# A hybrid SSD and latent-attention decoder on one core: a fourth pair in the second round of the FFN's products, a norm moved behind transposes, and rope queries transposed one value tile earlier

## The chip, the core and the metric

The kernel runs on one core of one Trainium2 chip. A core has TensorE (PE, with its weight loads listed as PEld), VectorE (DVE), ScalarE (ACT), GpSimd (POOL) and SyncE (SP), which here issues DMAs. Each works through its own list of instructions in order, and they meet at semaphores. The metric is device time in microseconds (us). Three runs of the kernel before gave 1320.35, 1320.42 and 1320.91, a median of 1320.42. The profile is of a further execution, which took 1320.28.

## The reference

A residual stream `h` of 512 tokens by 1024 goes through two layers. The first mixes tokens with a Mamba-2 scan (SSD), the second with multi-head latent attention (MLA, 8 heads, queries and keys with a rope part of 64). Behind each mixer stands a norm, then a gated FFN of 2816 hidden channels with a causal convolution over 3 tokens, then a norm again:

```python
for i in range(DEPTH):
    if i < N_A_LAYERS:
        mix = ssd_mixer(h, ...)
    else:
        mix = mla_attention(h, ..., k_nope, k_rope, v, cos, sin)
    h = layer_norm(DN_ALPHA * h + mix, ln_mix_g[i], ln_mix_b[i])
    ff = conv_ffn(h, ffn_up[i], ffn_conv_w[i], ffn_conv_b[i], ffn_down[i])
    h = layer_norm(DN_ALPHA * h + ff, ln_ffn_g[i], ln_ffn_b[i])
    if i == N_A_LAYERS - 1:
        shared_kv = mla_shared_kv(h, ...)

def conv_ffn(h, up, conv_w, conv_b, down):
    u = causal_depthwise_conv(h @ up, conv_w, conv_b)
    g, val = jnp.split(u, 2, axis=-1)
    return (jax.nn.silu(g) * val) @ down
```

All is float32.

## The kernel before, in words

**Products.** Every operand of a large product is split into a high part and the rest, and a product is three matmuls: high by high, high by rest, rest by high (`mm_a`, L159, and `mm_b`, L165 to L167). `h` stays on the chip as four token tiles of 128. Its transposed copy `ht` comes from `transpose_h` (L245): 8 transposes per token tile on PE, two casts on ACT (L248) for the high part, two subtractions on DVE (L249) for the rest.

**Weights.** `WStream` streams all weights in a fixed order: SP issues each load into one of 6 buffers (`wst`, L54), ACT casts it to `wh` (L96), DVE subtracts to get `wl` (L97); there are 6 pairs of `wh` and `wl`. A load waits until the split of the weights 6 loads ahead has freed its buffer. `ahead` splits weights before they are wanted, `retire` gives a pair back.

**The FFN** (`ffn`). Up projections go by pairs of 128 channels (`ci`, 22 in all, one for the gate and one for the value): PE's matmuls, then convolution, silu and gate on ACT and DVE (`conv3_silu_gate`). There are two rounds. Within a round hidden tiles are joined to pairs, and `RP` says how many pairs a round has and in which groups: 5 in the first, 3 in the second. A pair and its two halves of output and tokens are multiplied in a scheme of 7 products in place of 8 (`pair_operands` builds the sums of hidden tiles on DVE and ACT, `down_pairs` multiplies; the sums of weights are made in the buffers `rs`, by loads that POOL issues with addition, and on DVE). The results are added to `h` (L352, L353). The 6 hidden tiles that are in no pair go through the **tail**: for each token tile `piece` runs two halves of 512 outputs, 3 matmuls for each of the 6 tiles (36 matmuls of 512 columns a token tile), using weight tiles that hold two hidden tiles of one half (6 of them).

**The tail's norm.** Behind each half `add_mix` adds PE's sum to `h` on DVE (L185). Then `ln_apply` runs a chain over three engines: the negative mean on DVE (L192), the Square with its sum on ACT (L194), two small steps to the reciprocal root on POOL (L195, L196), the gain on DVE (L199, twice), the bias on DVE (L202, twice). L199 needs the gain and bias, which `load_ln` (L172) fetches into `lngb`, 1024 KB broadcast over the partitions; SP issues it when its turn comes in SP's list, ahead of the tail. In the first FFN `transpose_h(i-1)` stands between tile i's matmuls and its norm, so PE goes from tile i's matmuls to the transposes of tile i-1 and on to tile i+1. Tile 3's are left to `pend`, which the next stage flushes. In the last FFN nothing is transposed; tile 3 ends in `ln_last`, which splits its second half into 256 and 256 (L216, L222), and the output goes out by DMA.

**The scan's end** (the last lines of `ssd`). Its last two groups of heads go into `h` for tiles 0 to 3 (`out_part`, L185), each tile followed by its norm; tile 0 is transposed in the iteration of tile 2, tile 1 in that of tile 3, and tiles 2 and 3 by `pend`, after the first matmuls of the FFN on tiles 0 and 1.

**MLA.** `qk(h)` makes a head's queries and keys, `qk_rope(h)` transposes the rope queries of two heads (4 transposes, L1166) and splits them (L1171 on DVE), `v_tile(i, hf)` makes one half of a token tile of the values, `scores(h)` multiplies (L1183).

**What sets the order.** The program is written stage by stage, and when it is built the instructions of each engine are put into one list, by an estimate of when each can run. An edge on an engine (`tc.issue_after(x)`) puts instructions of x's engine behind x in its list.

Of the kernel before, what the change touches and what calls it, by code (L numbers as in the profile page):

```python
# [14 lines left out]
ALU = mybir.AluOpType  # L15
# [102 lines left out]
class K:  # L118
# [118 lines left out]
    def transpose_h(self, i):  # L237

        nc = self.nc
        ts = slice(i * P, (i + 1) * P)  # L240
        for q in range(2):
            b = self.bank()
            for j in range(4):
                k = q * 4 + j
                nc.tensor.transpose(b[:, j * P:(j + 1) * P], self.h[:, i, k * P:(k + 1) * P], self.ident)  # L245
            bv = b.rearrange("p (k t) -> p k t", k=4)
            hi = self.htt[:, q * 4:(q + 1) * 4, 0, ts]
            nc.scalar.copy(hi, bv)  # L248
            nc.vector.tensor_tensor(self.htt[:, q * 4:(q + 1) * 4, 1, ts], bv, hi, op=ALU.subtract)  # L249

    def flush(self):
        for f in self.pend:
# [2 lines left out]

RP = ((2, 2, 1), (1, 1, 1))
R0 = 2 * sum(RP[0])
R1 = R0 + 2 * sum(RP[1])  # L260


def ffn_items(up, down):
# [5 lines left out]
    for r, ks in enumerate((range(R0), range(R0, HT))):  # L269
# [4 lines left out]
        for odd, hf, kinds in ((0, 0, "r"), (0, 1, "a"), (1, 1, "+="), (0, 0, "-"), (1, 0, None), (1, 0, "a")):  # L274
            j = ks[0]
            for p, n in enumerate(RP[r]):
                b = dv[:, j:j + 2 * n, hf * 512:(hf + 1) * 512].rearrange("p (k e) n -> p k e n", e=2)[:, :, odd, :]
# [106 lines left out]
def ffn(k, ws, base, cwp, gb, la=2, out=None, mid=None):  # L384

    nc, tc = k.nc, k.tc
    with ExitStack() as c:
# [12 lines left out]
        for r in range(2):  # L400
# [49 lines left out]
            if mid and not r:  # L450
                mid()
            n = down_pairs(k, ws, n, prs, RP[r], not r)
        k.load_ln(gb)
# [72 lines left out]
def ssd(k, ws, base, xT, x, cwp, hv, ngp, gb):  # L526
    nc, tc = k.nc, k.tc
    with ExitStack() as cx:
# [327 lines left out]
        def out_part(g, i, stats=False, retire=None):  # L856

            assert "rs" in G[g]
            w = [ws.get(n[0] + OFF[g] + j, 4 - j) for j in range(2)]
            for hf in range(2):  # L860
                b = k.bank()
                o = slice(hf * 512, (hf + 1) * 512)
                for j in range(2):
                    k.mm_b(b, G[g]["yT"][j], slice(i * P, (i + 1) * P), w[j][0][:, o], w[j][1][:, o], j == 0, j == 1)
                    if retire and hf == 1:
                        ws.retire(n[0] + OFF[g] + j)
                k.add_mix(i, hf, b, rstd[:, g, i:i + 1], stats)
# [89 lines left out]
        for i in range(NT):  # L957
            if i >= 2:
                out_part(NG - 2, i, retire=i == NT - 1)
            if i == NT - 1:  # L960
                k.transpose_h(1)
            out_part(NG - 1, i, stats=True, retire=i == NT - 1)
            if i == NT - 1:
                n[0] += 4
                ws.ahead(n[0], 2)
            if i == 2:
                k.transpose_h(0)
            k.ln_apply(i)
    k.pend = [lambda: k.transpose_h(NT - 2), lambda: k.transpose_h(NT - 1)]
    return n[0]  # L970

# [65 lines left out]
def mla(k, ws, base, ngp, gb):  # L1037
    nc, tc = k.nc, k.tc
    with ExitStack() as cx:
# [76 lines left out]
        def v_tile(i, hf, retire=False):  # L1116
            b = k.bank()
            wh, wl = ws.get(n[0] + voff[0] + hf)
            for kk in range(2):
                k.mm_b(b, cT[3 + kk], slice(i * P, (i + 1) * P), wh[:, kk * 512:(kk + 1) * 512], wl[:, kk * 512:(kk + 1) * 512], kk == 0, kk == 1)  # L1120
            if not V:
                V["t"] = k.htp.tile([P, KT, 2, SEQ], F32R, name="ht")
            v = V["t"][:, 2 * i + hf]
            nc.scalar.copy(v[:, 0], b)
            nc.vector.tensor_tensor(v[:, 1], b, v[:, 0], op=ALU.subtract)
            V[i, hf] = v
# [18 lines left out]
        def qk(h, off=0):  # L1145
            S = H.setdefault(h, {})
            w = [v[:, :640].rearrange("p (k m) -> p k m", k=5) for v in ws.get(n[0] + off)]
            bq, bk = k.bank(), k.bank()
            k.mm_a(bq, [v[:, 0:3] for v in w], cT[:3], slice(0, SEQ))
            k.mm_a(bk, [v[:, 3:5] for v in w], cT[3:], slice(0, SEQ))  # L1150
            if not off:
                ws.retire(n[0])
                n[0] += 1
                ws.ahead(n[0])

            for nm, b, sc in (("q", bq, SCALE), ("k", bk, 1.0)):
                t = one.tile([P, 2, SEQ], F32R, name=f"{nm}T")
                nc.scalar.activation(t[:, 0], b, AF.Copy, scale=sc)
                nc.vector.scalar_tensor_tensor(t[:, 1], b, sc, t[:, 0], op0=ALU.mult, op1=ALU.subtract)
                S[nm] = t  # L1160

        def qk_rope(h):
            if h % 2 == 0:
                b = k.bank()
                for i in range(NT):
                    nc.tensor.transpose(b[:, i * P:(i + 1) * P], qr[:, i, h * RD:(h + 2) * RD], k.ident)  # L1166
                for e in range(2):
                    t = one.tile([P, SEQ], F32R, name=f"qrT{e}")
                    s = b[e * RD:(e + 1) * RD, :]
                    nc.scalar.activation(t[:RD], s, AF.Copy, scale=SCALE)  # L1170
                    nc.vector.scalar_tensor_tensor(t[RD:], s, SCALE, t[:RD], op0=ALU.mult, op1=ALU.subtract)  # L1171
                    H.setdefault(h + e, {})["r"] = t
# [83 lines left out]
        n[0] += 2  # L1256
        voff[0] = 0
        qk(0, 2)
        v_tile(NT - 1, 0)
        qk_rope(0)  # L1260
        v_tile(NT - 1, 1)
        for j in range(3):
            ws.retire(n[0] + j)
# [31 lines left out]
def trunk_kernel(tc, *aps):  # L1295
    d = dict(zip(_INS, aps))
    out = aps[len(_INS)]
    with ExitStack() as ctx:
        ctx.enter_context(tc.manual_schedule(engines={mybir.EngineType.SP}))
        k = K(tc, ctx)  # L1300
        items = ssd_items(d['xbc'], d['zdt'], d['zw'], d['sow'])
        items += ffn_items(d['up'][0], d['down'][0])
        items += mla_items(d['dw'], d['vw'], d['rw'], d['hw'], d['aow'])
        items += ffn_items(d['up'][1], d['down'][1])
        ws = WStream(k, items, k.nb, 3, k.la)
        n = ssd(k, ws, 0, d['xT'], d['x'], d['cw4'], d['hv'], d['sng'], d['gb'][0])
        n = ffn(k, ws, n, d['cw3'][0], d['gb'][1], la=5, mid=lambda: rope_tables(k, d['pos'], d['freq']))
        n = mla(k, ws, n, d['ang'], d['gb'][2])
        n = ffn(k, ws, n, d['cw3'][1], d['gb'][3], out=out)
# [53 lines left out]
```

## Time and profile before

| | before |
|---|---|
| runs, us | 1320.35, 1320.42, 1320.91 (median 1320.42) |
| profiled execution, us | 1320.28 |
| its span, us | 1318.6 |
| granted TensorE clock, mean | 0.998 |
| PE busy | 1309.1 us, 99% |
| DVE busy | 998.0 us, 76% |
| ACT busy | 633.1 us, 48% |
| POOL busy | 99.9 us, 8% |
| bytes moved | 143.55 MB, mean 109 GB/s |

How to read the lines that follow. The time line has start, duration, engine, source line, operation, output and inputs, shape, count; in brackets the idle time of the engine before and what ended it. Rows of several instructions are joined. The chain lists start, duration, engine and line of the work that ended last. A row of PE's waits is what waited, for which engine and line, us in total, times, longest. A row of windows has the stretch, its length, then busy time and count of PE, PEld, DVE, ACT and POOL, the granted clock, the share of the DMA engines and GB/s. Times are from the start of the span.

The stages that the change touches lie here: the scan's end at 415 to 434, the first FFN's second round of up projections before 713, its products at 713 to 742, its tail at 742 to 777, MLA's first scores at 835, and the last FFN's tail from about 1279 to the end at 1318.6.

### The profile page before, as it was taken

How to read it: one execution, taken by the hardware profiler on the slowest of the kernel's cores; microseconds unless marked ns; L12 is line 12 of the kernel's file. 1: busy time of each engine (PE TensorE's matmuls, PEld its weight loads, DVE VectorE, ACT ScalarE, POOL GpSimd, SP SyncE). 2: the span in 40 equal slices, each digit the busy share in tenths (PEclk: the TensorE clock that was granted, in tenths of full speed). 3: DMA queues.
4: the chain of work that ended last, by engine and by line, in shares of the span. 5: the costliest groups of instructions: out<-in, count | busy, mean ns of one | idle time of the engine just before them, and what ended most of it. 6: DMA issues, size and time to landing. Idle time of an engine off the chain costs nothing.

```text
span 1318.6 us, 17522 instructions
## 1 busy us (share of the span) xinstructions
PE 1309.1 (99%) x6740; PEld 1106.3 (84%) x6740; DVE 998.0 (76%) x1539; ACT 633.1 (48%) x1030; POOL 99.9 (8%) x98
## 2 busy tenths in 40 slices
PE   9999999999999999999999999999999999999997
PEld 8888888888888988888888899888898888888886
DVE  7788898787798868866757776887577686666585
ACT  6665555446453544444443444665254444444341
POOL 0111011001011001000001022000100010000001
PEclk9999999999999999999999999999999999999999
DMA  8422313313410533352311721321044217332151
GB/s 295 178 112 113 120 45 140 128 58 132 163 65 1 179 128 81 80 205 98 112 48 33 247 86 61 111 82 33 32 147 136 80 31 216 128 96 81 33 176 64
DMA packets 49108, 143.55 MB, mean 109 GB/s; under 512 B 5344, under 2 KB 6368, under 8 KB 47488
## 3 DMA queue, kind: packets, MB, share of 16 engines
q1 hardware_dynamic: 44544, 134.04, 29.5%
q0 software_dynamic: 4480, 8.39, 3.9%
q8 instruction: 53, 0.87, 0.3%
q14 instruction: 31, 0.25, 0.1%
HBM read 140.25 MB, written 2.16 MB: 108 GB/s over the span
## 4 chain that ended last, share of the span: by engine, by line
PE 98%; DVE 1%; issue 0%; ACT 0%; DVEq 0%; ACTq 0%
PE ps L159 57%; PE ps L165 10%; PE ps L167 10%; PE ps L166 10%; PE ps L1183 2%; PE ps L733 1%; PE ps L1217 1%; PE ps L841 1%; PE ps L741 1%; PE ps L245 1%; PE ps L722 1%; PE ps L700 1%; PE ps L1204 1%; PE ps L674 1%; DVE wl L97 0%; PE ps L554 0%
## 5 line engine op out<-in xcount | busy, mean ns | idle before, releaser
L159 PE MATMUL ps<-ht,wh 128*128 128x512 f32 (+1 forms) x2272 | 518.7, 378 | 0.7 <-ACT ht L248 0.4
L159 PEld LDWEIGHTS ps<-ht,wh 128*128 128x128 f32 x2272 | 409.0, 188 | 79.9 <-ACT ht L248 0.8
L97 DVE TENSOR_TENSOR wl<-wst,wh 128x1024 fp32r<-128x1024 f32 (+4 forms) x226 | 254.9, 1145 | 38.3 <-ACT wh L96 38.0
L159 PE MATMUL ps<-ht,wl 128*128 128x512 f32 (+1 forms) x1136 | 267.3, 377 | 0.0
L96 ACT CAST wh<-wst 128x1024 fp32r<-128x1024 f32 (+4 forms) x226 | 219.9, 984 | 94.3 <-PE ps L167 48.8
L159 PEld LDWEIGHTS ps<-ht,wl 128*128 128x128 f32 x1136 | 205.9, 188 | 39.4
L293 DVE SCALAR_TENSOR_TENSOR acc<-ps,cw,acc 128x511 f32<-128x511 f32 x88 | 65.7, 747 | 81.9 <-ACT acc L292 81.9
L165 PE MATMUL ps<-wh,gt 128*128 128x512 f32 (+1 forms) x326 | 125.9, 386 | 0.0
L167 PE MATMUL ps<-wh,gt 128*128 128x512 f32 (+1 forms) x326 | 125.6, 385 | 0.0
L166 PE MATMUL ps<-wl,gt 128*128 128x512 f32 (+1 forms) x326 | 125.6, 385 | 0.0
L589 DVE SCALAR_TENSOR_TENSOR cv<-ps,cw,cv 128x511 f32<-128x511 f32 (+2 forms) x96 | 71.2, 745 | 34.1 <-ACT cv L587 33.5
L305 ACT CAST gt<-acc 128x512 fp32r<-128x512 f32 (+1 forms) x76 | 42.3, 574 | 101.9 <-DVE acc L298 98.8
L292 ACT ACTIVATE acc<-ps,cw 128x512 f32<-128x512 f32 x88 | 68.3, 776 | 35.0 <-PE ps L159 35.0
L165 PEld LDWEIGHTS ps<-wh,gt 128*128 128x128 f32 x326 | 61.2, 188 | 12.7 <-issue 0.5
L166 PEld LDWEIGHTS ps<-wl,gt 128*128 128x128 f32 x326 | 61.3, 188 | 12.2
L167 PEld LDWEIGHTS ps<-wh,gt 128*128 128x128 f32 x326 | 61.2, 188 | 12.2
L294 DVE SCALAR_TENSOR_TENSOR acc<-ps,cw,acc 128x510 f32<-128x510 f32 x88 | 65.8, 748 | 2.4
L297 ACT ACTIVATE acc<-acc 128x512 f32<-128x512 f32 x44 | 27.8, 632 | 82.5 <-DVE acc L294 82.2
L52 POOL DMA_DIRECT2D rs<-in_down_dram x24 | 23.8, 991 | 567.3 <-DVE wl L97 434.4
L96 ACT CAST wh<-rs 128x512 fp32r<-128x512 f32 (+1 forms) x48 | 36.6, 763 | 46.7 <-DVE rs L88 23.3
L306 DVE TENSOR_TENSOR gt<-acc,gt 128x512 fp32r<-128x512 f32 (+1 forms) x76 | 46.8, 631 | 14.0 <-ACT gt L305 14.0
L352 DVE SCALAR_TENSOR_TENSOR h<-h,ps 128x512 f32<-128x512 f32 x56 | 36.9, 684 | 21.7 <-PE ps L167 21.7
(240 smaller groups left out, 1750.0 us busy)
## 6 DMA issues: line engine op xcount, KB each, us to landing
wst<-in_up_dram SPq DMA_DIRECT2D x88, 512.0 KB, 3.5
wst<-in_xbc_dram SPq DMA_DIRECT2D x32, 512.0 KB, 6.2
wst<-in_down_dram SPq DMA_DIRECT2D x24, 512.0 KB, 5.6
W<-cumd SPq DMA_DIRECT2D x8, 1024.0 KB, 4.7
wst<-in_sow_dram SPq DMA_DIRECT2D x16, 512.0 KB, 4.6
wst<-in_zw_dram SPq DMA_DIRECT2D x14, 512.0 KB, 6.8
wst<-in_down_dram SPq DMA_DIRECT2D x24, 256.0 KB, 2.7
lngb<-in_gb_dram SPq DMA_DIRECT2D x4, 1024.0 KB, 7.2
```

What stands on the lines that cost most here:

```text
L96: nc.scalar.copy(h[:, :f], s[:, :f])
L97: nc.vector.tensor_tensor(l[:, :f], s[:, :f], h[:, :f], op=ALU.subtract)
L159: nc.tensor.matmul(out, w[:, k, :], xts[k][:, x, ts], start=first and p == 0 and k == 0, stop=last and p == 2 and k == nk - 1, skip_group_ ...
L165: nc.tensor.matmul(out, xt[:, 0, tsl], wh, start=start, stop=False, skip_group_check=True)
L166: nc.tensor.matmul(out, xt[:, 0, tsl], wl, start=False, stop=False, skip_group_check=True)
L167: nc.tensor.matmul(out, xt[:, 1, tsl], wh, start=False, stop=stop, skip_group_check=True)
L292: nc.scalar.activation(a, b, AF.Identity, bias=cw[:, ch, 3:4], scale=cw[:, ch, 2:3])
L293: nc.vector.scalar_tensor_tensor(a[:, 1:], b[:, :SEQ - 1], cw[:, ch, 1:2], a[:, 1:], op0=ALU.mult, op1=ALU.add)
L294: nc.vector.scalar_tensor_tensor(a[:, 2:], b[:, :SEQ - 2], cw[:, ch, 0:1], a[:, 2:], op0=ALU.mult, op1=ALU.add)
L305: k.nc.scalar.copy(dst[:, 0, :], src)
L306: k.nc.vector.tensor_tensor(dst[:, 1, :], src, dst[:, 0, :], op=ALU.subtract)
L589: nc.vector.scalar_tensor_tensor(t[:, d:], b[:, :SEQ - d], cw[:, ch, 3 - d:4 - d], t[:, d:], op0=ALU.mult, op1=ALU.add)
```

## The change

Three edits. The line numbers of the changed kernel are higher by 1 to 5 behind `transpose_h`.

```diff
@@ transpose_h
-            nc.scalar.copy(hi, bv)
-            nc.vector.tensor_tensor(self.htt[:, q * 4:(q + 1) * 4, 1, ts], bv, hi, op=ALU.subtract)
+            a = nc.scalar.copy(hi, bv)
+            v = nc.vector.tensor_tensor(self.htt[:, q * 4:(q + 1) * 4, 1, ts], bv, hi, op=ALU.subtract)
+        return a, v
@@
-RP = ((2, 2, 1), (1, 1, 1))
+RP = ((2, 2, 1), (2, 1, 1))
@@ ssd, end
             if i == NT - 1:
-                k.transpose_h(1)
+
+                a, v = k.transpose_h(1)
+                with tc.issue_after(a.ins), tc.issue_after(v.ins):
+                    k.ln_apply(2)
             out_part(NG - 1, i, stats=True, retire=i == NT - 1)
...
             if i == 2:
                 k.transpose_h(0)
-            k.ln_apply(i)
+            else:
+                k.ln_apply(i)
@@ mla
         qk(0, 2)
+        qk_rope(0)
         v_tile(NT - 1, 0)
-        qk_rope(0)
         v_tile(NT - 1, 1)
```

**`RP`.** The second round of each FFN takes 8 hidden tiles in 4 pairs instead of 6 in 3. The tail of each FFN has 4 hidden tiles in place of 6, so 24 matmuls per token tile and 4 weight tiles. Nothing else in the FFN is edited, but the lists of the engines change with it. In the first FFN's tail ACT's list was this; `lnst` and `lnjunk` belong to the norms of tiles 0, 1 and 2, `ht` to the transposed tiles, `wh` to weights of the next stage:

```order
L194 ACTIVATE lnjunk_6461,lnst_6438<-h_93,lnst_6438 128x1024
L248 CAST ht_6412<-ps_6510 128x4x128
L248 CAST ht_6412<-ps_6517 128x4x128
L194 ACTIVATE lnjunk_6525,lnst_6488<-h_93,lnst_6488 128x1024
L248 CAST ht_6412<-ps_6574 128x4x128
L248 CAST ht_6412<-ps_6581 128x4x128
L194 ACTIVATE lnjunk_6589,lnst_6552<-h_93,lnst_6552 128x1024
L96 CAST wh_6610<-wst_6364 128x1024
L96 CAST wh_6625<-wst_6370 128x1024
```

and with the change:

```order
L194 ACTIVATE lnjunk_6502,lnst_6485<-h_93,lnst_6485 128x1024
L248 CAST ht_6465<-ps_6539 128x4x128
L248 CAST ht_6465<-ps_6546 128x4x128
L194 ACTIVATE lnjunk_6554,lnst_6523<-h_93,lnst_6523 128x1024
L248 CAST ht_6465<-ps_6591 128x4x128
L248 CAST ht_6465<-ps_6598 128x4x128
L96 CAST wh_6630<-wst_6411 128x1024
L194 ACTIVATE lnjunk_6606,lnst_6575<-h_93,lnst_6575 128x1024
L96 CAST wh_6642<-wst_6417 128x1024
```

The first cast of the next stage's weights (`wh_6630`) now stands ahead of tile 2's Square; it stood behind it.

In the last FFN, DVE's list at tile 3 was this (`lnst_11279` and `lnlast_11319` are its sums):

```order
L185 SCALAR_TENSOR_TENSOR h_93,lnst_11279<-h_93,ps_11260 128x512
L216 SCALAR_TENSOR_TENSOR h_93,lnlast_11319<-h_93,ps_11281 128x256
L217 TENSOR_SCALAR lnlast_11319<-lnlast_11319,lnst_11279 128x1
L218 TENSOR_SCALAR lnlast_11319<-lnlast_11319 128x1
L220 TENSOR_SCALAR lnst_11279<-lnlast_11319 128x1
L221 TENSOR_SCALAR lnst_11279<-lnlast_11319 128x1
L222 SCALAR_TENSOR_TENSOR h_93,lnlast_11319<-h_93,ps_11282 128x256
L225 TENSOR_SCALAR lnst_11279<-lnlast_11319,lnst_11279 128x1
L226 TENSOR_SCALAR lnst_11279<-lnst_11279 128x1
L227 TENSOR_SCALAR lnlast_11319<-lnst_11279,lnlast_11319 128x1
L228 TENSOR_SCALAR lnst_11279<-lnlast_11319,lnst_11279 128x1
```

and with the change:

```order
L185 SCALAR_TENSOR_TENSOR h_93,lnst_11271<-h_93,ps_11258 128x512
L216 SCALAR_TENSOR_TENSOR h_93,lnlast_11299<-h_93,ps_11273 128x256
L222 SCALAR_TENSOR_TENSOR h_93,lnlast_11299<-h_93,ps_11274 128x256
L217 TENSOR_SCALAR lnlast_11299<-lnlast_11299,lnst_11271 128x1
L218 TENSOR_SCALAR lnlast_11299<-lnlast_11299 128x1
L220 TENSOR_SCALAR lnst_11271<-lnlast_11299 128x1
L225 TENSOR_SCALAR lnst_11271<-lnlast_11299,lnst_11271 128x1
L227 TENSOR_SCALAR lnlast_11299<-lnst_11271,lnlast_11299 128x1
L221 TENSOR_SCALAR lnst_11271<-lnlast_11299 128x1
L226 TENSOR_SCALAR lnst_11271<-lnst_11271 128x1
L228 TENSOR_SCALAR lnst_11271<-lnlast_11299,lnst_11271 128x1
```

The last add, L222, stands right behind L216, ahead of the five small steps that it stood behind or among.

**The scan's end.** Tile 2's norm is written behind tile 1's transposes. On ACT its Square stands behind the last of their casts, and on DVE it stands behind the last of their subtractions. DVE's list was this, where `lnst_3778` is tile 2, `lnst_3854` tile 3, the first two L249 tile 0's transposes and the later two tile 1's:

```order
L249 TENSOR_TENSOR ht_3696<-ps_3788,ht_3696 128x4x128
L249 TENSOR_TENSOR ht_3696<-ps_3795,ht_3696 128x4x128
L192 TENSOR_SCALAR lnst_3778<-lnst_3778 128x1
L185 SCALAR_TENSOR_TENSOR h_93<-ps_3811,rstd_112,h_93 128x512
L185 SCALAR_TENSOR_TENSOR h_93<-ps_3819,rstd_112,h_93 128x512
L97 TENSOR_TENSOR wl_3842<-wst_3645,wh_3841 128x1024
L199 SCALAR_TENSOR_TENSOR h_93<-h_93,lnst_3778,lngb_3399 128x512 x2
L202 SCALAR_TENSOR_TENSOR h_93<-h_93,lnst_3778,lngb_3399 128x512 x2
L249 TENSOR_TENSOR ht_3696<-ps_3827,ht_3696 128x4x128
L249 TENSOR_TENSOR ht_3696<-ps_3834,ht_3696 128x4x128
L185 SCALAR_TENSOR_TENSOR h_93,lnst_3854<-ps_3847,rstd_112,h_93 128x512
```

and with the change:

```order
L249 TENSOR_TENSOR ht_3696<-ps_3788,ht_3696 128x4x128
L249 TENSOR_TENSOR ht_3696<-ps_3795,ht_3696 128x4x128
L185 SCALAR_TENSOR_TENSOR h_93<-ps_3802,rstd_112,h_93 128x512
L185 SCALAR_TENSOR_TENSOR h_93<-ps_3810,rstd_112,h_93 128x512
L249 TENSOR_TENSOR ht_3696<-ps_3818,ht_3696 128x4x128
L249 TENSOR_TENSOR ht_3696<-ps_3825,ht_3696 128x4x128
L192 TENSOR_SCALAR lnst_3778<-lnst_3778 128x1
L97 TENSOR_TENSOR wl_3842<-wst_3645,wh_3841 128x1024
L185 SCALAR_TENSOR_TENSOR h_93,lnst_3854<-ps_3847,rstd_112,h_93 128x512
L199 SCALAR_TENSOR_TENSOR h_93<-h_93,lnst_3778,lngb_3399 128x512 x2
L202 SCALAR_TENSOR_TENSOR h_93<-h_93,lnst_3778,lngb_3399 128x512 x2
L185 SCALAR_TENSOR_TENSOR h_93,lnst_3854<-ps_3856,rstd_112,h_93 128x512
```

Tile 1's two L249 went ahead of tile 2's mean (L192), and tile 2's L199 and L202 went behind the first add of tile 3.

**MLA.** The rope queries of heads 0 and 1 are transposed and split ahead of the first half of the last value tile, rather than between its halves. PE's four transposes go ahead of six matmuls, and ACT's and DVE's steps with them; no DMA moves.

## The prediction

> **What bounds the kernel now.** I read the page's head, its busy times and its chain by engine first, then the chain in order of time, then PE's own waits.
>
> ```profile
> span 1318.6 us, 17522 instructions
> PE 1309.1 (99%) x6740; PEld 1106.3 (84%) x6740; DVE 998.0 (76%) x1539; ACT 633.1 (48%) x1030; POOL 99.9 (8%) x98
> PE 98%; DVE 1%; issue 0%; ACT 0%; DVEq 0%; ACTq 0%
> ```
>
> ```profile
> 1.10 4.21 PE ps L554 x18
> ...
> 582.82 130.56 PE ps L159 x576
> ...
> 758.39 0.87 PE ps L245 x8
> 767.44 0.87 PE ps L245 x8
> 776.53 0.87 PE ps L245 x8
> ...
> 960.40 8.63 PE ps L159 x72
> ```
>
> ```profile
> PE ps L1183 <- DVE qrT L1171: 0.5, 1, 0.5
> PE ps L159 <- ACT ht L248: 0.4, 1, 0.4
> PE ps L159 <- DVE ht L249: 0.3, 1, 0.3
> ```
>
> PE is the bound: 1309.1 of 1318.6 us busy, 98% of the chain, and what it waits for sums to little. So there are three prices: a 512-wide matmul is 130.56 / 576 = 0.2267 us, a 256-wide one 8.63 / 72 = 0.120, and any wait that lands on PE counts in full. The three rows of 8 transposes are tiles 0 to 2 in the first FFN's tail: one period is 9.05 us, which less 0.87 is 8.18, or 36 matmuls (8.16). That tail runs without a gap on PE. Only in the last 7.1 us does PE have nothing left.
>
> The change buys PE time with DVE's cover. The stages to read are therefore the two tails, where one token tile's matmuls are what hides one token tile's norm.
>
> **Matmuls saved.** In each FFN the tail loses two hidden tiles: 2 x 3 products x 4 token tiles x 2 halves = 48 matmuls (in the last FFN 6 of them are 12 of half width). The fourth pair adds 7 products x 3 x 2 = 42. First FFN: -6 x 0.2267 = **-1.36**. Last FFN: -42 x 0.2267 - 12 x 0.120 + 42 x 0.2267 = **-1.44**. The product stage grows by 42 x 0.2267 = 9.52, and a token tile of a tail falls from 36 matmuls (8.16) to 24 (**5.44**).
>
> **The wider product stage.** The windows of the second round's up projections and of its products in the first FFN (PE, PEld, DVE, ACT, POOL busy):
>
> ```profile
> 648.00:670.00 22.00, 22.00 (x99) 18.23 (x98) 15.76 (x22) 10.44 (x15) 0.00 (x0) 1.00 0.31 96
> 713.40:741.90 28.50, 28.50 (x127) 23.39 (x126) 25.84 (x39) 15.78 (x23) 2.60 (x3) 1.00 0.60 174
> ```
>
> The fourth pair's operands and its wider weight sums and splits go to DVE. It is idle 6.24 of 22 us in the first window, and only 2.66 of 28.5 in the second, where PE gets 9.52 longer. I take 0 and keep up to 0.3 for a split that comes late; the cover is PE's added matmuls, and without it the DVE work would be paid in full.
>
> **First FFN's tail.** DVE's rows, SP's issue of the norm's gain and bias (lngb), its landing, and ACT's first cast at the last tile:
>
> ```profile
> 750.26 0.69 DVE L185 SCALAR_TENSOR_TENSOR h<-h,ps 128x512 f32<-128x512 f32 x1 [2.94 <-PE ps L167]
> ...
> 753.73 1.41 DVE L199 SCALAR_TENSOR_TENSOR h<-h,lnst,lngb 128x512 f32<-128x512 f32 x2 [2.52 <-DMA lngb<-in_gb_dram]
> 755.06 1.41 DVE L202 SCALAR_TENSOR_TENSOR h<-h,lnst,lngb 128x512 f32<-128x512 f32 x2
> ```
>
> ```profile
> 746.13 0.38 SPq L172 DMA_DIRECT2D lngb<-in_gb_dram  x1
> ```
>
> ```profile
> DMA to landing us min/median/max: 7.5/7.5/7.5
> ```
>
> ```profile
> 772.52 1.05 ACT L96 CAST wh<-wst 128x1024 fp32r<-128x1024 f32 x1 [0.31 <-PE ps L167]
> ```
>
> The tail begins 72 matmuls ahead of the first transposes, at about 741.9; times from there are t. Before, lngb was issued at t = 4.2 and DVE waited for it until 11.8. Nobody saw that, since tile 0's transposes came only at t = 16.3 (72 x 0.2267). Now they are due at 2 x 5.44 = t 10.9. SP's order is unchanged: lngb stands behind a weight load whose buffer comes free at the second of the last three splits, and those splits stand where they stood. I put the issue 0.5 earlier, so lngb lands at 3.7 + 7.5 = 11.2. L199 then takes until 12.5 (755.06 - 753.73 = 1.33), the first half of L202 until 13.3, the second until 13.95. PE stalls **2.7** at tile 0.
>
> Everything behind moves with it. On DVE tile 1's mean (L192) now stands behind tile 0's L249s, so tile 1's norm starts some 3 us into the 5.44 it has: **0.5**. At tile 2 the cast of the next weights stands ahead of the Square on ACT. Like the quoted cast it waits for PE to free a tail buffer, 6 matmuls (1.36) into tile 3, and the Square waits with it: **1.3**. Sum 4.5, net **+3.1**. From below: lngb at 10.5 gives stalls of 3.8 (+2.4). If it did not bind at all, tiles 0 to 2 would still lose 2.3 (+0.95). From above: an issue no earlier and one late split (11.8 to 12.5) gives 5.1 to 5.8 (+4.4).
>
> **Last FFN's tail.** DVE's rows, and PE's last:
>
> ```profile
> 1286.82 0.69 DVE L185 SCALAR_TENSOR_TENSOR h<-h,ps 128x512 f32<-128x512 f32 x1 [2.94 <-PE ps L167]
> ...
> 1294.98 0.69 DVE L185 SCALAR_TENSOR_TENSOR h<-h,ps 128x512 f32<-128x512 f32 x1 [1.95 <-PE ps L167]
> ...
> 1297.29 1.41 DVE L199 SCALAR_TENSOR_TENSOR h<-h,lnst,lngb 128x512 f32<-128x512 f32 x2 [1.37 <-ACT lnjunk L194]
> 1299.15 1.42 DVE L202 SCALAR_TENSOR_TENSOR h<-h,lnst,lngb 128x512 f32<-128x512 f32 x2 [0.45 <-POOL lnst L196]
> 1300.48 0.68 DVE L185 SCALAR_TENSOR_TENSOR h<-h,ps 128x512 f32<-128x512 f32 x1
> ...
> 1308.65 0.68 DVE L185 SCALAR_TENSOR_TENSOR h<-h,ps 128x512 f32<-128x512 f32 x1
> 1309.37 0.42 DVE L216 SCALAR_TENSOR_TENSOR h<-h,ps 128x256 f32<-128x256 f32 x1
> ```
>
> ```profile
> 1311.21 0.28 PE L167 MATMUL ps<-wh,gt 128*128 128x256 f32 x1
> ```
>
> From a tile's second add to the next tile's first add DVE takes 1300.48 - 1294.98 = 5.50, the two waits for ACT and POOL in it included, since the adds stand behind L202. With 0.67 for one more add its cycle is **6.17 a tile**. That was under 8.16 and is over 5.44: DVE becomes the bound of this tail. From tile 0's second add, tile 1's first comes 5.5 later, tile 2's second at 6.17 x 2 = 12.3, tile 3's first at 12.36 + 5.50 = 17.9. Before it was 1308.65 - 1286.82 = 21.8. So 4.0 is gained behind that add, and some 0.27 more (an estimate, from L222's 0.42 less the 0.15 of L221 beside it) since tile 3's last add, L222, now stands ahead of the small steps and finds PE done. Tile 0 is 12 matmuls earlier (-2.72) and the products are 9.52 longer: 9.52 - 2.72 - 4.24 = **+2.56**, where PE alone would give -1.44. Bounds: +1.9 if one add of the next tile slips into the 1.37 wait (0.67 less, once), +3.0 if a split ahead of tile 0 comes one 0.45 late.
>
> **Scan's end.** PE's rows, and DVE's at tile 3:
>
> ```profile
> 422.39 1.24 PE L159 MATMUL ps<-ht,wh 128*128 128x256 f32 x8 [0.41 <-ACT ht L248]
> ...
> 426.28 0.74 PE L159 MATMUL ps<-ht,wh 128*128 128x256 f32 x4 [0.26 <-DVE ht L249]
> ...
> 431.65 2.11 PE L245 MATMUL ps<-ident,h 128*128 128x128 f32 x16
> ```
>
> ```profile
> 429.78 1.42 DVE L199 SCALAR_TENSOR_TENSOR h<-h,lnst,lngb 128x512 f32<-128x512 f32 x2 [1.37 <-ACT lnjunk L194]
> 431.63 1.41 DVE L202 SCALAR_TENSOR_TENSOR h<-h,lnst,lngb 128x512 f32<-128x512 f32 x2 [0.43 <-POOL lnst L196]
> ```
>
> Tile 1's casts no longer stand behind tile 2's norm, so the 0.41 and 0.26 go. But of the 16 transposes at 431.65 the last 8 read tile 3 behind L202: its first half is done at about 431.63 + 0.75 = 432.4, and they are due at 431.65 + 8 x 0.11 = 432.5. They are already as late as tile 3's norm lets them be. DVE's work stays the same, and POOL's pow is alone on its queue; what stands behind the moved mean on DVE is one weight split, wanted several us later, and tile 3's adds and norm. Those cannot start sooner, and tile 2's norm, begun later, leaves its waits for ACT and POOL less covered. If PE arrives 0.7 earlier it waits 0.6 there. I take **+0.2**: from -0.1 (some matmuls slip between) to +0.6 (both gaps bare).
>
> **Rope.** PE's row and DVE's:
>
> ```profile
> 835.44 0.33 PE L1183 MATMUL ps<-ka,qrT 128*128 128x128 f32 x1 [0.45 <-DVE qrT L1171]
> ```
>
> ```profile
> 834.70 0.68 DVE L1171 SCALAR_TENSOR_TENSOR qrT<-ps,qrT 64x512 fp32r<-64x512 f32 x1
> ```
>
> The four transposes and DVE's L1171 go ahead of six matmuls (1.36), and the 0.45 goes; the gap of starts is 0.1 more. A little may come back at the transposed probabilities. **-0.55**, from -0.65 to 0 (all of it comes back).
>
> **Sum.** +3.1 + 2.56 + 0.2 - 0.55 = +5.3 on the profiled execution's 1320.28, its span and 1.7 around it: 1325.6. It lies 0.14 under the median of the runs, 1320.42, so **1325.8**. The mechanism's own range is 1324.0 to 1327.5. What can be told from no change is 0.2%, 2.6 us.
>
> **The skill on the largest term.** The Trainium skill ("DMA: Bandwidth & Descriptors", "Anatomy of one DMA — SWDGE (gpsimd) path") fits a DMA by 2.0 us + bytes / 436 GB/s: by estimate 4.4 us for these 1024 KB, if it held for SP's queue too. The row says 7.5. By the Trainium skill's fit lngb would land at t = 8.1 and the sum would be 1323.6; the measured row decides.
>
> **Rivals.**
>
> *The load is in time* (0.13). Tile 0's L199 could start at t = 5.6 + 2.3 = 7.9 (1297.29 - 1294.98 in the last tail). If the splits before the tail run 3 us sooner, lngb lands by then; the first tail then costs +0.95: 1323.6. For it: 6.24 us of idle DVE in the up projections. Against: 2.66 in the products, and the unchanged place of lngb.
>
> *One tail pays alone* (0.10). Either the first keeps its -1.36 (1321.3) or the last its -1.44 (1321.8): within 0.2%. Against it: each tail fails by its own rows.
>
> *Faster: both tails stay with PE* (0.07). One mechanism: DVE's cycle a tile falls under 5.44, because adds and means go ahead while it waits 1.37 and 0.45, and lngb is there by t = 8. 6.17 less 1.82 is 4.35, so the room exists; it decides below 5.44. Then -2.80 - 0.55 + 0.2: 1317.3. Against: in the last tail the row order leaves both waits bare.
>
> *The clock falls* (0.06). PE's idle time in the first tail comes near 3 us in one piece.
>
> ```profile
> 1311.50:1318.60 7.10, 0.00 (x0) 0.00 (x0) 4.01 (x11) 0.60 (x2) 0.98 (x1) 0.71 0.20 74
> ```
>
> After PE's last matmul the granted clock averages 0.71 over 7.1 us: if it is full and then half, full for 3.0 us (3.0 + 4.1 / 2 = 0.71 x 7.1). The first 18 matmuls of the program, from rest, took 4.21 us, 0.234 each, about twice the 0.87 / 8 = 0.109 of the 128-wide transposes. If lngb is 0.6 later still, the stall passes 3.0 and half of some 4.2 us is lost: 1325.8 + 0.6 + 2.1 = 1328.5. The Trainium skill ("TensorE: Matmul & The Clock Gate", "Why this matters for your kernels") says that idle gaps of PE over about 3.4 us halve its clock; the end of this trace agrees with about 3 us. By the Trainium skill's figure a stall of 2.7 costs nothing more than itself.
>
> **Chances.** Forecast 0.64, in time 0.13, one tail 0.10, faster 0.07, clock 0.06. Slower by over 0.2%: 0.64 + 0.06 + 0.11 of the 0.13, whose lower bounds reach 1322.4, = 0.81; within 0.12; faster 0.07. The range leaves out the faster case, most of one tail, and the clock: 1322.4 to 1328.0.
>
> **What would show it.** Right: L199 of the first tail's tile 0 still waits for lngb, and PE's L245 waits for DVE there, 2 to 3 us; in the last tail DVE's second adds are 6.2 apart and PE's end comes about 11 us before the span's; the 0.41, 0.26 and 0.45 are gone, and a wait stands before the transposes at the scan's end. Wrong: transposes 5.44 + 0.87 = 6.3 apart without waits, or second adds 5.4 apart.

## The result, and the profile after

| | before | after |
|---|---|---|
| median, us | 1320.38 (6 runs, 1320.01 to 1320.99) | 1326.16 (6 runs, 1325.12 to 1327.01) |
| ratio | | 1.0042, 95% interval 1.0029 to 1.0055 |
| profiled execution / span, us | 1320.28 / 1318.6 | 1326.16 / 1324.5 |

The changed kernel is 5.8 us slower. The forecast was 1325.8. The page of the changed kernel, its head, busy times and chain by engine:

```profile
span 1324.5 us, 17479 instructions
...
PE 1307.0 (99%) x6722; PEld 1103.3 (83%) x6722; DVE 1008.4 (76%) x1547; ACT 637.6 (48%) x1030; POOL 98.0 (7%) x98
...
PE 62%; DVE 3%; DMA 1%; issue 1%; ACT 0%; POOL 0%; DVEq 0%; SPq 0%; ACTq 0%
```

PE is busy 2.1 us less than before, and the span is 5.9 longer: matmuls were saved and waits were bought. DVE and a DMA now stand in the chain, which the profile follows back to 432.13 only, so that its shares sum to 67%. Where the time went is read by laying the same PE instruction of both time lines side by side:

| start of the same PE instruction | before | after | shift | of which new |
|---|---|---|---|---|
| first matmul behind the start-up | 19.00 | 19.49 | +0.49 | +0.49 |
| first matmul behind the scan end's transposes | 433.51 | 434.01 | +0.50 | +0.01 |
| first product, second round, first FFN | 713.21 | 713.71 | +0.50 | 0.00 |
| first matmul of MLA | 777.15 | 781.41 | +4.26 | **+3.76** |
| first matmul behind head 1's scores | 857.89 | 861.62 | +3.73 | **-0.53** |
| first product, second round, last FFN | 1249.74 | 1253.49 | +3.75 | +0.02 |
| end of PE's last matmul | 1311.49 | 1313.64 | +2.15 | **-1.60** |
| end of the span | 1318.6 | 1324.5 | +5.9 | **+3.75** |

The first row is no part of the change: it is the start of the program, which waits for its first weights, and it scattered from +0.1 to +1.2 over all the kernels below. Runs of one kernel differ by about as much. So the experiments are read by stages, with their own first matmul as the origin.

PE's waits with the change:

```profile
PE ps L245 <- DVE h L202: 4.9, 3, 2.8
PE ps L555 <- DVE warm L135: 1.1, 1, 1.1
PE ps L842 <- ACT wh L96: 0.2, 1, 0.2
```

The 0.5, 0.4 and 0.3 of before are gone, as the two small edits meant. In their place PE waits 4.9 us at three groups of transposes for the bias step. One of the three stands at the scan's end, two lie in the first FFN's tail, here in PE's time line:

```profile
433.03 1.23 PE L245 MATMUL ps<-ident,h 128*128 128x128 f32 x8 [1.03 <-DVE h L202]
...
765.64 1.32 PE L245 MATMUL ps<-ident,h 128*128 128x128 f32 x8 [2.81 <-DVE h L202]
...
772.50 1.32 PE L245 MATMUL ps<-ident,h 128*128 128x128 f32 x8
...
780.34 1.32 PE L245 MATMUL ps<-ident,h 128*128 128x128 f32 x8 [1.04 <-DVE h L202]
```

In the tail before, a group looked like this:

```profile
758.23 1.03 PE L245 MATMUL ps<-ident,h 128*128 128x128 f32 x8
```

The eight transposes took 1.03 before and take 1.32 now: the second four wait 0.29 for the second half of L202. DVE's rows there, and lngb's issue and landing:

```profile
758.16 0.21 DVE L192 TENSOR_SCALAR lnst<-lnst 128x1 f32<-128x1 f32 x1
760.15 0.69 DVE L185 SCALAR_TENSOR_TENSOR h<-h,ps 128x512 f32<-128x512 f32 x1 [1.77 <-PE ps L167]
...
763.50 1.41 DVE L199 SCALAR_TENSOR_TENSOR h<-h,lnst,lngb 128x512 f32<-128x512 f32 x2 [2.66 <-DMA lngb<-in_gb_dram]
764.84 1.41 DVE L202 SCALAR_TENSOR_TENSOR h<-h,lnst,lngb 128x512 f32<-128x512 f32 x2
```

```profile
755.45 0.42 SPq L172 DMA_DIRECT2D lngb<-in_gb_dram  x1
```

```profile
DMA to landing us min/median/max: 8.0/8.0/8.0
```

PE's first tail matmul starts at 751.78, so lngb is issued at t = 3.7 and lands at 11.7. DVE had waited for it 2.5 us before as well (the row was in the profile of before); what is new is that PE waits behind DVE.

In the last FFN's tail, DVE's rows, and PE's last matmul:

```profile
1297.21 0.69 DVE L185 SCALAR_TENSOR_TENSOR h<-h,ps 128x512 f32<-128x512 f32 x1 [2.02 <-PE ps L167]
...
1303.34 0.68 DVE L185 SCALAR_TENSOR_TENSOR h<-h,ps 128x512 f32<-128x512 f32 x1
...
1305.65 1.42 DVE L199 SCALAR_TENSOR_TENSOR h<-h,lnst,lngb 128x512 f32<-128x512 f32 x2 [1.37 <-ACT lnjunk L194]
1307.51 1.41 DVE L202 SCALAR_TENSOR_TENSOR h<-h,lnst,lngb 128x512 f32<-128x512 f32 x2 [0.45 <-POOL lnst L196]
...
1309.45 0.68 DVE L185 SCALAR_TENSOR_TENSOR h<-h,ps 128x512 f32<-128x512 f32 x1
...
1315.55 0.41 DVE L216 SCALAR_TENSOR_TENSOR h<-h,ps 128x256 f32<-128x256 f32 x1
```

```profile
1313.36 0.28 PE L167 MATMUL ps<-wh,gt 128*128 128x256 f32 x1
```

Second adds stand 6.13, 6.11 apart, without a wait for PE behind the first one, where before each had waited almost 2 us for PE. DVE reaches tile 3's first 256 columns (L216) at 1315.55, 1.9 us after PE's last matmul; before it was there 2.1 us ahead of its end.

### The profile page after: what moved, and what is told of

Its sections match the earlier page's. It is cut to its first block, busy times and chain, and to the rows that moved or that the text cites. A ratio compares the mean times of both kernels' runs of the same rounds, so it can differ in the third digit from the quotient of the medians.

```text
span 1324.5 us, 17479 instructions
## 1 busy us (share of the span) xinstructions
PE 1307.0 (99%) x6722; PEld 1103.3 (83%) x6722; DVE 1008.4 (76%) x1547; ACT 637.6 (48%) x1030; POOL 98.0 (7%) x98
## 4 chain that ended last, share of the span: by engine, by line
PE 62%; DVE 3%; DMA 1%; issue 1%; ACT 0%; POOL 0%; DVEq 0%; SPq 0%; ACTq 0%
PE ps L159 37%; PE ps L167 7%; PE ps L165 7%; PE ps L166 7%; PE ps L1188 2%; PE ps L1222 1%; PE ps L245 1%; PE ps L1209 1%; DMA lngb<-in_gb_dram 1%; DVE wl L97 1%; DVE h L202 1%; DVE h L185 0%; ACT lnjunk L194 0%; POOL lnst L196 0%; PE ps L1109 0%
## 5 line engine op out<-in xcount | busy, mean ns | idle before, releaser
L97 DVE TENSOR_TENSOR wl<-wst,wh 128x1024 fp32r<-128x1024 f32 (+3 forms) x222 | 253.9, 1158 | 39.5 <-ACT wh L96 38.4
L96 ACT CAST wh<-wst 128x1024 fp32r<-128x1024 f32 (+3 forms) x222 | 218.6, 995 | 102.2 <-PE ps L167 52.6
L165 PE MATMUL ps<-wh,gt 128*128 128x512 f32 (+1 forms) x320 | 123.8, 387 | 0.0
L167 PE MATMUL ps<-wh,gt 128*128 128x512 f32 (+1 forms) x320 | 123.7, 386 | 0.0
L96 ACT CAST wh<-rs 128x1024 fp32r<-128x1024 f32 (+1 forms) x48 | 40.1, 835 | 51.2 <-DVE rs L88 27.2
```

What stands on the lines that cost most here:

```text
L96: nc.scalar.copy(h[:, :f], s[:, :f])
L97: nc.vector.tensor_tensor(l[:, :f], s[:, :f], h[:, :f], op=ALU.subtract)
L165: nc.tensor.matmul(out, xt[:, 0, tsl], wh, start=start, stop=False, skip_group_check=True)
L167: nc.tensor.matmul(out, xt[:, 1, tsl], wh, start=False, stop=stop, skip_group_check=True)
```

## The experiments

Two theories stood at the start. **Cover**: a tail gains from fewer matmuls only while the norm of one tile still ends inside PE's time for the next; at 24 matmuls it doesn't, in the first tail for lngb and the lists, in the last for DVE's 6.13 a tile. **Elsewhere**: the loss comes from the wider products or from the two other edits. Shifts are by stage, against the profiled execution of before, as in the table above: first FFN (products to MLA), rope, last FFN (products to the end of the span). The ratio is to runs of the kernel before on the same chip. The last column scatters by up to 0.2 where nothing in that FFN was edited. That scatter is the output's store: from DVE's last step to the end of the span it took 2.8 to 3.2 us over these kernels, while DVE's last step itself comes at the same time to 0.02 where nothing was edited. By DVE's last step the changed kernel's last FFN is at +1.92.

| kernel | median, us | against before | first FFN | rope | last FFN |
|---|---|---|---|---|---|
| changed kernel | 1326.16 | 1.0042 [1.0029, 1.0055] | +3.76 | -0.53 | +2.15 |
| e1_pairs_only | 1326.79 | 1.0047 [1.0032, 1.0062] | +2.83 | -0.04 | +2.15 |
| e2_scan_only | 1320.74 | 0.9997 [0.9987, 1.0007] | +0.03 | +0.01 | 0.00 |
| e3_rope_only | 1320.40 | 0.9997 [0.9987, 1.0006] | +0.03 | -0.51 | -0.01 |
| e4_first_ffn_only | 1324.60 | 1.0031 [1.0019, 1.0043] | +4.73 | -0.02 | +0.14 |
| f1_lngb_early | 1320.66 | 0.9997 [0.9988, 1.0006] | **-1.46** | -0.51 | +1.81 |
| f2_last_tail_order | 1326.18 | 1.0040 [1.0028, 1.0053] | +3.49 | -0.49 | +1.34 |
| f3_all_tails | 1319.77 | 0.9993 [0.9984, 1.0001] | -1.46 | -0.52 | +0.99 |
| f4_order_three_pairs | 1320.96 | 1.0002 [0.9993, 1.0010] | 0.00 | 0.00 | +0.34 |
| h1_first_ffn_early | 1319.06 | 0.9984 [0.9975, 0.9993] | -1.46 | -0.47 | +0.22 |
| h2_no_bias_step | 1317.64 | 0.9973 [0.9963, 0.9984] | -1.46 | -0.52 | **-1.60** |
| h3_early_old_order | 1323.06 | 1.0015 [1.0006, 1.0024] | +1.00 | -0.52 | +1.79 |
| h4_early_three_pairs | 1321.09 | 0.9999 [0.9990, 1.0008] | +0.01 | 0.00 | +0.19 |

### Which edit costs

**e1_pairs_only.** The kernel before with

```diff
-RP = ((2, 2, 1), (1, 1, 1))
+RP = ((2, 2, 1), (2, 1, 1))
```

> The kernel before with the fourth pair in both FFNs and nothing else. Theory (the two tails lose their cover): first FFN +3.8, last FFN +2.1, so +5.9, 1326.3; PE waits for L202 three times in the first tail (4.9 in all), DVE's second adds are 6.13 apart in the last. Rival (the other two edits carry part of the loss, say the moved norm disturbs the weight stream): under +4.5, 1324.9 or less.

1326.79: the pairs alone bring the whole loss. PE waits for L202 twice, 2.9 us in all, not three times: the third wait of the changed kernel belongs to the scan's end, which is as before here. The first FFN was expected at +3.8 and costs 0.9 less than in the changed kernel, with the same order in that tail. The difference is the landing of lngb, 7.0 us in place of 8.0:

```profile
762.88 1.41 DVE L199 SCALAR_TENSOR_TENSOR h<-h,lnst,lngb 128x512 f32<-128x512 f32 x2 [1.73 <-DMA lngb<-in_gb_dram]
```

DVE waits 1.73 for it and PE 1.88 behind DVE, against 2.66 and 2.81. What the load takes more goes into the time one for one.

**e2_scan_only.** The edits in `transpose_h` and at the end of `ssd`, with `RP` and the rope queries as before.

> The kernel before with tile 2's norm behind tile 1's transposes and nothing else. Theory (tile 3's norm ends the stage whatever stands ahead of it): 0.0, between -0.2 and +0.3, with a wait of about 1.0 between the transposes of tile 2 and of tile 3. Rival (the two waits that it removes, 0.41 and 0.26, are gained and the wait at tile 3 came only with the pairs): -0.7.

1320.74, and no stage moved: 0.04 us at the scan's end. The waits of 0.41 and 0.26 went, and one came:

```profile
PE ps L245 <- DVE h L202: 1.0, 1, 1.0
```

It stands between the transposes of tile 2 and tile 3. The rival, -0.7, is out: tile 3's norm ends that stage.

**e3_rope_only.** `qk_rope(0)` ahead of `v_tile(NT - 1, 0)`, all else as before.

> The kernel before with the rope queries ahead of the last value tile and nothing else. Theory: the wait of 0.45 goes for good, -0.5. Rival (it comes back at the transposed probabilities): 0.0, with a wait of PE of 0.4 there.

1320.40. The interval of the runs can't tell this from no change, but the time line can: -0.51 at that place, and nothing given back.

**e4_first_ffn_only.** The kernel before, with `RP` chosen for each FFN:

```diff
+PAIRS = {False: ((2, 2, 1), (2, 1, 1)), True: ((2, 2, 1), (1, 1, 1))}
...
 def ffn(k, ws, base, cwp, gb, la=2, out=None, mid=None):
...
+    RP = PAIRS[out is not None]
+    R1 = R0 + 2 * sum(RP[1])
```

> The kernel before with the fourth pair in the first FFN alone. Theory: its own tail costs what it costs, +3.8, 1324.2, and the last FFN is as before, with 7.1 us behind PE's last matmul. Rival (each FFN loses the same 3.0 in its products, where DVE gets more work): +3.0, and the time from the first product to the first tail matmul longer than 28.7 + 9.5.

1324.60. The rival is out: from the first product to the first tail matmul it takes 38.1 us, as in every kernel here with four pairs, under the rival's 38.2, and the last FFN is as before (+0.14, in the store). In its profiled execution the first FFN costs +4.73, though PE's waits are shorter than in the changed kernel. PE's busy time, clock, DMA share and GB/s, stretch by stretch around tile 0's transposes:

```profile
757.00:762.90 5.90, 5.90 (x28) 1.00 0.83 302
762.90:765.40 2.50, 0.30 (x3) 1.00 0.02 9
765.40:766.30 0.90, 0.89 (x6) 1.00 0.00 0
766.30:769.70 3.40, 3.40 (x11) 0.50 0.00 0
769.70:774.00 4.30, 4.24 (x20) 1.00 0.00 0
```

PE stood still for 2.2 us and soon after ran 3.4 us at half its clock, a loss of about 1.7. That was the prediction's clock rival, at a shorter idle time than the 3.0 it was given. In the changed kernel 2.8 us in one piece left the clock at 1.00, so the length alone doesn't decide. The Trainium skill ("TensorE: Matmul & The Clock Gate", "Why this matters for your kernels") gives over about 3 us as the gap to avoid; this run disagrees, a gap of 2.2 was enough once.

What decides can be read from the granted clock in the traces. In all 14 profiled executions it changes only on a grid of 3.413 us: full clock lasts 1307.31 or 1310.72 us in one piece (383 or 384 steps of the grid), and here 761.17, then 3.41 at half, then 549.55 (223, 1 and 161 steps). PE's busy time in the steps with the gap, here and then in the changed kernel:

```profile
762.88:766.29 3.41, 1.21 (x8) 1.00 0.02 7
```

```profile
761.17:764.58 3.41, 1.66 (x8) 1.00 0.27 109
764.58:768.00 3.42, 2.36 (x14) 1.00 0.00 0
```

The gap of 2.2 lay in one step and left PE busy for 35% of it, and the next step ran at half clock. The gap of 2.8 fell across two steps, which stayed 49% and 69% busy, and cost no clock. Over the 14 traces each step at full clock with PE busy for 35% or less is followed by half clock, and none with 48% or more. The grid lies elsewhere in each execution (full clock begins 4.1 to 7.2 us into the span), so the same gap can cost 1.7 us in one execution and nothing in the next. How much of the scatter between runs this makes stays open: the runs of the four kernels with a gap of about 2 us or more range over 1.6 to 2.3 us, those of the other edited kernels over 0.7 to 1.8, and the changed kernel's profiled execution, at its median of 1326.16, has no step at half clock before PE's end.

### The first tail

**f1_lngb_early.** The changed kernel with

```diff
...
-        k.load_ln(gb)
+        k.load_ln(gb, nc.gpsimd)
```

in `ffn`, where the second argument, which `load_ln` takes in the part left out, is the engine that issues the load.

> The changed kernel with one edit: in both FFNs lngb is fetched through POOL's DMA queue, which is idle there, instead of SP's, so that it no longer stands behind weight loads and lands before the tail's first norm. Theory (in the first tail lngb decides at tile 0, the norm's chain at the other tiles): 2.3 of the 5.1 us of PE's waits there stay, so -2.8 against the changed kernel, 1323.4. Rival (DVE's list decides; the load only stood in front of it): the waits move to tiles 1 and 2, -1.0 at most, 1325.2. The last FFN is unchanged by both.

1320.66, twice the gain that was expected. The load and PE's three groups of transposes:

```profile
L172 POOL DMA_DIRECT2D lngb<-in_gb_dram x1: 564/564/564, 743.8 to 743.8; - x1
...
DMA to landing us min/median/max: 4.9/4.9/4.9
```

```profile
762.63 1.07 PE L245 MATMUL ps<-ident,h 128*128 128x128 f32 x8
...
769.02 1.03 PE L245 MATMUL ps<-ident,h 128*128 128x128 f32 x8
...
775.36 1.04 PE L245 MATMUL ps<-ident,h 128*128 128x128 f32 x8
```

lngb is issued 11.6 us earlier and lands in 4.9. The Trainium skill's fit ("DMA: Bandwidth & Descriptors", "Anatomy of one DMA — SWDGE (gpsimd) path") gives 4.4 for this size by estimate, and this row of POOL's queue is near it; in h4_early_three_pairs below the same load took 7.1 on POOL's queue. All of PE's waits in that tail are gone, its groups stand 6.4 apart (24 matmuls and 8 transposes), and the first FFN gives the full -1.46. DVE's second adds stand 6.13 and 6.11 apart there, as in the changed kernel's last tail: with its transposes PE's time a tile, 6.4, still covers that, where the last tail's 5.44 does not. So the theory's 2.3 us of remaining waits did not remain. They came from the lists: with the load early, the lists that the build makes differ. DVE has tile 0's L199 and L202 ahead of tile 1's first add, tile 1's mean ahead of the L249s, and ACT has tile 2's Square ahead of the cast:

```profile
770.65 1.15 ACT L194 ACTIVATE lnjunk<-h,lnst 128x1024 bf16<-128x1024 f32 x1
...
771.80 2.12 ACT L96 CAST wh<-wst 128x1024 fp32r<-128x1024 f32 x2
```

**h3_early_old_order** tests that. It is f1_lngb_early with the changed kernel's lists held by edges:

```diff
+                with tc.issue_after(k.mix.ins):
+                    k.ln_scale(i - 1, k.sc)
...
+                a, v = k.transpose_h(i - 1)
+                with tc.issue_after(v.ins):
+                    k.ln_stats(i)
```

`ln_stats` is the mean, Square and root, `ln_scale` the gain and bias, `k.mix` the add of tile i's first half.

> f1_lngb_early, with the lists of DVE and ACT in the first tail held to those of the changed kernel: the next tile's first add ahead of the gain and bias steps, a tile's mean behind the subtractions of the tile before, the next weights' cast ahead of tile 2's Square. Theory now (the late load cost twice, once by itself and once by the lists that were built around it): 2.3 of PE's waits come back, 1323.0. Rival (the lists cost nothing once the load is there): 1320.7.

1323.06: 2.46 of waits came back with lngb long there. At tile 2, in ACT's and PE's time lines:

```profile
772.49 1.05 ACT L96 CAST wh<-wst 128x1024 fp32r<-128x1024 f32 x1 [0.84 <-PE ps L167]
773.44 1.15 ACT L210 ACTIVATE lnjunk<-h,lnst 128x1024 bf16<-128x1024 f32 x1
```

```profile
777.53 1.32 PE L265 MATMUL ps<-ident,h 128*128 128x128 f32 x8 [1.03 <-DVE h L221]
```

The Square (here L210) stands behind the cast, the cast waits for PE, and PE then waits 1.03 for the norm. So the late load cost twice: 3.76 - 1.00 = 2.76 by itself, and 1.00 + 1.46 = 2.46 through the lists that were built around it.

**h4_early_three_pairs.** The control: the kernel before with f1's edit.

> A control: the kernel before, with three pairs, with only lngb through POOL's queue. Theory: with 36 matmuls a tile the load was hidden, so 0.0. Rival (the earlier load itself speeds up the kernel): -2 or more.

1321.09, and the first FFN's stage is the same to 0.01. With 36 matmuls a tile the late load was free. The load's own row here:

```profile
L172 POOL DMA_DIRECT2D lngb<-in_gb_dram x1: 564/564/564, 737.0 to 737.0; - x1
...
DMA to landing us min/median/max: 7.1/7.1/7.1
```

It took 7.1 us on POOL's queue, with weights moving beside it (314 to 381 GB/s in all). In f1_lngb_early it took 4.9 at 214 GB/s, which is the load alone, and in the changed kernel's last FFN 4.5 on SP's queue at 233 GB/s, again alone. So POOL's queue is not the faster one: what f1_lngb_early gains is the earlier issue, and a landing beside less traffic.

### The last tail

**f2_last_tail_order.** The changed kernel, where in the last FFN a tile's gain and bias follow the next tile's second add (its first add at tile 3):

```diff
...
+                v, old = k.mix, sc
+                k.ln_stats(i)
+                sc = k.sc
+                if i:
+                    scale_out(i - 1, old, v)
...
```

`scale_out` is `ln_scale` behind an edge on `v`, and the two output DMAs. At tile 3 the part left out calls it for tile 2 behind tile 3's first add.

> The changed kernel with one edit: in the last FFN's tail a tile's gain and bias steps stand on DVE behind the adds of the next tile, so the waits for ACT and POOL are covered by PE's next 5.4 us. Theory (DVE's list with its bare waits is the bound of that tail, 6.13 a tile; its work alone is 4.1): PE becomes the bound again, about 7 us behind its last matmul, the last FFN goes from +2.15 to -1.4 against before, 1322.6. Rival (the tail is bound by the amount of norm work over the engines): no gain, 1326.2.

1326.18, a miss: the last FFN gained 0.8 of the 3.6 expected. DVE's rows (L221 is gain and bias):

```profile
1302.19 0.69 DVE L185 SCALAR_TENSOR_TENSOR h<-h,ps 128x512 f32<-128x512 f32 x1 [2.02 <-PE ps L167]
1302.80 0.75 DVE L221 SCALAR_TENSOR_TENSOR h<-h,lnst,lngb 128x512 f32<-128x512 f32 x1
...
1311.62 2.73 DVE L221 SCALAR_TENSOR_TENSOR h<-h,lnst,lngb 128x512 f32<-128x512 f32 x4
1314.28 0.41 DVE L236 SCALAR_TENSOR_TENSOR h<-h,ps 128x256 f32<-128x256 f32 x1
```

The wait for ACT is covered, but DVE now idles 2.02 ahead of an add with the previous tile's steps already runnable behind it, and tile 2's four steps (2.73) stand between tile 3's adds, where PE's results lie ready. The work was pushed to the end, where nothing covers it.

**f3_all_tails** is f1_lngb_early and f2_last_tail_order together, with edges that keep in the first tail each mean ahead of the L249s and the casts behind tile 2's Square.

> The changed kernel with both edits (lngb through POOL's queue, the last tail's gain and bias behind the next adds) and in the first tail each tile's mean ahead of the subtractions of the tile before, and the next stage's weight casts behind tile 2's Square. Theory: both tails go back to PE's pace, the first with up to 0.8 of waits, so the fewer matmuls count at last: -2.8 - 0.5 + 0.5, 1317.6. Rival (something else that the fourth pair brought holds PE, in the products or at the end): above 1320.

1319.77, of which the first FFN gives its -1.46 and the last still costs +0.99 (by DVE's last step +1.11, as in f2_last_tail_order). The expected 1317.6 falls with f2's term.

**f4_order_three_pairs.** The control: f2's edit on the kernel before.

> A control: the kernel before, with three pairs, with only the last tail's new order on DVE. Theory: with 36 matmuls a tile PE covers DVE either way, so 0.0, at most -0.3 from the order of the last small steps. Rival (the order itself is faster, whatever the cover): -3.5, as in the changed kernel.

1320.96: no gain in the runs. The 0.34 in the last FFN is not the store's scatter: DVE's last step comes 0.36 later, so with three pairs the new order costs a little. Here too tile 2's four steps stand between tile 3's adds.

**h2_no_bias_step.** Since an order that covers everything was not found, the work was taken away instead: f1_lngb_early without L202 at tiles 0 to 2 of the last FFN (those tokens leave without the root factor and the bias).

```diff
...
-            k.ln_apply(i)
+            k.ln_apply(i, out is None)
```

> f1_lngb_early with the bias step (L202) of tiles 0 to 2 left out in the last FFN, so that DVE's time a tile falls from 6.13 by 1.33 and the wait of 0.45 to about 4.3, under PE's 5.44. Theory (the last tail loses because DVE's time a tile is over PE's): PE's pace comes back, second adds 5.4 apart, about 7.2 us behind the last matmul, the last FFN at -1.5 against before, 1317.3. Rival (what is lost comes after the last matmul whatever stands ahead of it): 1320.5.

1317.64. DVE's second adds:

```profile
1291.94 0.69 DVE L185 SCALAR_TENSOR_TENSOR h<-h,ps 128x512 f32<-128x512 f32 x1 [2.02 <-PE ps L167]
...
1297.38 0.69 DVE L185 SCALAR_TENSOR_TENSOR h<-h,ps 128x512 f32<-128x512 f32 x1 [1.10 <-PE ps L167]
...
1302.82 0.69 DVE L185 SCALAR_TENSOR_TENSOR h<-h,ps 128x512 f32<-128x512 f32 x1 [1.10 <-PE ps L167]
```

They are 5.44 apart and wait for PE again, and the last FFN stands at -1.60, which is PE's saving (by DVE's last step -1.48, the rest is the store). The products, which are the same, cost nothing beyond their matmuls.

### What beats both

**h1_first_ffn_early.** The changed kernel, with e4's `PAIRS` (the fourth pair in the first FFN alone) and f1's load in that FFN.

> The changed kernel, but with the fourth pair in the first FFN alone, where lngb comes through POOL's queue; the last FFN keeps three pairs. Theory (a stage gains its fewer matmuls only where the norm's chain of a tile still ends within PE's time for the next): -1.46 in the first FFN, -0.5 at the rope queries, 0.0 in the last FFN, so -2.0 against before, 1318.9. Rival (lngb by POOL or the other mix costs elsewhere): no better than f1_lngb_early, 1320.7.

1319.06, 0.9984 of before with an interval below 1: each FFN has the number of pairs that its tail can cover.

## Why the prediction was right, point by point

- **The bound and the prices.** PE's saving was forecast at -1.36 and -1.44; where all cover holds, the stages show -1.46 and -1.60. Up to the first tail matmul the products grew by 9.39, forecast 9.52. The wider products and their operands were put at 0, and h2_no_bias_step shows 0.
- **First FFN's tail**, the largest term: +3.1 forecast, +3.76 measured. The issue of lngb was forecast at t = 3.7 and came there. The landing took 8.0 in place of the 7.5 of before (7.0 and 7.3 in e1 and e4), and the second four transposes of each group wait 0.29 more, three times, which the sum does not name. Against f1_lngb_early, which has no waits there, PE's first group starts 2.96 later (2.7 in the sum), the second another 0.47 (0.5), the third another 1.50 (1.3), and the last group ends 0.29 later. The sum's 0.5 was for a wait ahead of tile 1's group, where PE's row lists none; most of the 0.47 is the 0.29 within tile 0's. The lower bound's 2.3 without the load is h3's 2.46. It held for those lists only; that the lists themselves follow from the load's time was not seen, and is why f1_lngb_early was under-forecast.
- **Last FFN's tail**: +2.56 forecast, +2.15 measured. The cycle was 6.17 in the sum and 6.13 on the chip; PE's end came 10.8 us ahead of the span's, forecast 11. By DVE's last step it is +1.92. The difference lies mostly behind tile 3's first add, where the new order of the small steps gave 0.63 in place of the 0.27 in the sum.
- **Scan's end**: +0.2 forecast, 0.0 measured, inside its bounds. The wait moved to tile 3's transposes, 1.03 against the 0.6 given.
- **Rope**: -0.55 forecast, -0.5 measured.
- **Rivals.** *The load is in time* did not happen, but f1_lngb_early shows what it would have given: -1.46 in the first FFN, where the rival put +0.95, since the lists changed with it. *One tail pays alone* and *faster* failed on the rows that were quoted against them. *The clock falls* happened in one profiled execution of e4, at a shorter idle time than forecast. The 3.0 us that the prediction took from the end of the trace of before was one draw: over the 14 traces half clock sets in 2.2 to 5.2 us after PE's last matmul, wherever the grid puts it. The section of the Trainium skill that the prediction names for 3.4 us has about 3.
- **The sum.** It fits better than its terms, and that is partly luck: by stages the change costs +5.4, forecast +5.3, with errors of 0.66 in the first tail, -0.41 in the last, -0.2 at the scan's end and 0.05 at the rope queries that nearly cancel. On the median the terms add to 1325.7, not 1325.8, and one tail to 1321.7, not 1321.8. All lower bounds together give the 1324.0 of the mechanism's range; all upper ones give 1328.4, not 1327.5.

Left open: whether some order of DVE's list lets the last tail run at PE's pace with the full norm. DVE's own work a tile (two adds, a mean, four steps: 0.67 x 6 + 0.12 = 4.1) would fit in 5.44; the one order tried did not do it.

## What to carry to other kernels

Before removing work from the bottleneck engine, find the stages where that work is the cover of something else, and compare the two per tile: what is left (5.44 us, or 6.4 with the transposes) against the longest chain that must end inside it (6.13, or a load that lands at 11.7). A wait in the trace that costs nothing, like DVE's 2.52 for lngb before, is the first to cost something when its cover shrinks, and fixing it first (an earlier issue of one load, on an engine whose list did not hold it up) was worth 5.2 us here, more than the matmuls saved. When a planner builds the lists, a late transfer costs a second time through the order that is built around it.

## What the runs showed of the hardware that was not expected

- The same 1024 KB load took 7.0 to 8.0 us on SP's queue and 7.1 on POOL's (h4_early_three_pairs) beside weight loads (260 to 340 GB/s in all), and 4.5 on SP's and 4.9 on POOL's when nothing else moved.
- The granted clock changed only on a grid of 3.413 us, in all 14 traces, and fell to half behind a step with PE busy for 35% or less, never behind one with 48% or more. An idle stretch of 2.2 us within one step cost 1.7 us (e4_first_ffn_only); one of 2.8 us across two cost nothing (the changed kernel).
- The start of the program, which no edit touched, moved by up to 1.2 us between executions, more than two of the three edits are worth; the stages behind it repeat to about 0.04 us, and the output's store at the end took 2.8 to 3.2.
